# First gate pairs interleaved with their moving sums, three groups of elementwise work given to GpSimd, in a hybrid encoder layer on one core

## The chip, the cores and the metric

The kernel runs on one core of a Trainium2 chip. The metric is the device time of one execution in microseconds (us). Engines are called PE (TensorE), DVE (VectorE), ACT (ScalarE), POOL (GpSimd) and SP (SyncE).

## The reference

One layer of an encoder on 1024 tokens of width 1024, with 16 meta tokens ahead of them. What the change touches is the z part of the first projection, the two merge gates, and the gate/up projection of the SwiGLU:

```python
h = rmsnorm(h_res, norm1_w)
proj = h @ w_in
(q, k, v, z, b_raw, a_raw, sc_b, sc_c, sc_x, gate_a, gate_b) = split(proj)
o_dn = gated_deltanet_bidir(q, k, v, z, b_raw, a_raw, ...)   # gated by silu(z)
y_a = o_dn @ w_branch_dn
y_b = (sc_b * depthwise_conv_centred(sc_c * sc_x, sc_conv_w)) @ w_branch_sc
merged = sigmoid(gate_a) * y_a + sigmoid(gate_b) * y_b
h_res = h_res + merged @ w_out
h2 = rmsnorm(h_res, norm2_w)
gu = h2 @ w_gate_up
h_res = h_res + (silu(gu[..., :D_FF]) * gu[..., D_FF:]) @ w_down
out = rmsnorm(h_res, final_norm_w)[:, N_META:]
```

Everything is float32.

## The kernel before

**Arithmetic.** Each float32 operand of a large matmul is split in two: ACT casts a high part (`CAST`, L101 in `split`), DVE subtracts it from the value to get a low part (L102). Three matmuls per block of 128 rows give the product (high by high, high by low, low by high). `dense` (24 matmuls, 128x512 each) is such a product over eight blocks.

**Gate pairs.** The two merge gates are computed in pairs of units: for unit j = 3 to 7 (`GH` to `KT - 1`, n = 0 to 4), a block of gate A and one of gate B make one 2x2 block product with the 2x2 blocks B11, B12, B21, B22 of the activations. It is done with seven products instead of eight. On the weights' side stand A11, A12, A22 and sums S1 to S4; on the activations' side B11, B21, B22 and sums T1 to T4. `product` (12 matmuls, 128x512 each, L1440) is one of them. `pair_weights` loads a pair's raw weights (tiles `raw`) and gives two functions: `first` splits A11 and A12 (`wh`, `wl`), `second` splits A22 (`u_hl`; tile `w` for pair 0), forms S1 to S4 on DVE in place (`sums`, tiles `raw`) and splits these into tiles `mB` for even n and `mA` for odd n (`stationary2`). `pair` issues the products and combines the banks into two output tiles `s`. In order: A11·B11 and A12·B21 (both left half of the first output), S2·T2, S1·T1, S3·T3, S4·B22, A22·T4; the bank of A11·B11 is used again by S2·T2, S3·T3 and A22·T4.

**Moving sums.** `moving_sums` is a generator that forms T1 to T4 once, in steps, from high and low parts of the activations: float32 sums on DVE (128x2048, in tiles `mA` and `b`), the high CAST on ACT (L1457), and the low part on DVE (`b`). The tile `d_` holds differences of the low parts, once for T1 and again for T3.

**z heads.** `z_rows` does the last three heads of z (z0, z1, z2): two halves each, every one a `dense` into a bank from `psany`, then ACT's tanh of half (L1502) and on DVE one operation that reads the bank and ends the gate (L1504). `psany` rotates over all eight PSUM banks (tags m: two, e: three, d: three); `psz` rotates over m and e, `pss` gives d.

**Order.** From the z heads to the end of pair 0 the order on DVE, PE and ACT is the order of the source (`manual_schedule`, `border0`), and so it is on DVE alone in gate/up block 0. Elsewhere a list scheduler orders instructions when the program is built. Each engine runs its instructions strictly in that order.

**Gate/up.** The same scheme runs on the SwiGLU's projection. While the last row blocks are normalised and transposed, `second_half` forms the sums for T1, T2, T3 for a range of columns, `split_T2` splits T2 (`mA`) in two slices of columns (384 and 128 of each of four blocks, so 1536 and 512 elements a partition), and `form_T4` makes T4's float32 value in place of T2's with two operations on DVE (L179 and L228, tile `al`). T4's high CAST on ACT (`b`) and its low split on DVE follow.

Of the kernel before, what the change touches and what calls it, by code (L numbers as in the profile page):

```python
# [8 lines left out]
F32 = mybir.dt.float32  # L9
# [9 lines left out]
KT = 8  # L19
# [29 lines left out]
def encoder_layer(ctx: ExitStack, tc: tile.TileContext, x, meta, norm1_w, w_in, w_ba,  # L49
# [128 lines left out]
    def sub(out, a, b):  # L178
        nc.vector.tensor_tensor(out=out, in0=a, in1=b, op=ALU.subtract)  # L179
# [29 lines left out]
    def second_half(c, pts):  # L209
# [5 lines left out]
        sub(t2, b22, t1)  # L215
        sub(t3, b22, pts[0])

    def split_T2(c):

        b21h, b21l = (m[:, :, c].bitcast(F32) for m in mov["B21"])  # L220
        t2 = m32[2][:, :, c]
        split(*(m[:, :, c] for m in mov["T2"]), t2)

    def form_T4(c):
        b21h, b21l = (m[:, :, c].bitcast(F32) for m in mov["B21"])
        t2 = m32[2][:, :, c]
        sub(t2, b21h, t2)
        nc.vector.tensor_tensor(out=t2, in0=t2, in1=b21l, op=ALU.add)  # L228


    p_d = [dr.tile([P, SEQ], F32, name=f"p_d{i}") for i in range(KT)]
# [804 lines left out]
    with tc.tile_pool(name="st", bufs=1) as st:  # L1036
# [374 lines left out]
    s_hl, u_hl = [None, None], [None, None]  # L1411
    mov = {}

    def sums(rg, ru, s2, s4_, s3, s1):
        g0, g1, u0, u1 = rg[:, 0:4], rg[:, 4:8], ru[:, 0:4], ru[:, 4:8]
        nc.vector.tensor_tensor(out=s1, in0=u0, in1=u1, op=ALU.add)
        sub(s3, g0, u0)
        sub(s2, s1, g0)
        sub(s4_, g1, s2)

    def stationary2(j, ru, sa, sb, A_):

# [19 lines left out]
    def moving_sums():  # L1442

        c = [slice(C0 + META + 512 * i, C0 + META + 512 * i + 512) for i in range(2)]
        f = lambda m: m.bitcast(F32)
        h0, h1 = ([f(hx[0][:, 4 * i:4 * i + 4, cc]) for cc in c] for i in range(2))
        l0, l1, l2 = ([f(t[:, :, cc]) for cc in c] for t in low_tiles)
        for i in range(2):
            for j in range(2):
                mov[f"B{i + 1}{j + 1}"] = hx[0][:, 4 * i:4 * i + 4, c[j]], [hx[1][4 * i + k][:, c[j]] for k in range(4)]  # L1450
        for i, n in enumerate(("T1", "T2", "T3")):
            t = big(f"b{i}", [P, 2, 4, 512])
            mov[n] = t[:, 0], t[:, 1]
# [3 lines left out]
        high = lambda n, t: nc.scalar.copy(mov[n][0], t)  # L1457
# [12 lines left out]
        low_part("T2", t2)  # L1470
        yield
        sub(t3, h1[1], h0[1])
        sub(d_[:, a], l1[1], l0[1][:, a])
        sub(d_[:, b], l2[1], l0[1][:, b])
        add(t3, t3, d_)
        high("T3", t3)
        yield
        sub(t1, h1[0], t2)
        low_part("T3", t3)
        yield  # L1480
        t = big("b3", [P, 2, 4, 512])
# [14 lines left out]
    def z_rows(h):  # L1496

        sz = s4(SEQ)
        for sl in (left, right):
            po = psany()  # L1500
            dense(po, z_units[h - ZH], hx, C0 + META + sl.start, 512)
            nc.scalar.activation(sz[:, sl], po, AF.Tanh, scale=0.5)  # L1502
            yield
            nc.vector.scalar_tensor_tensor(out=sz[:, sl], in0=sz[:, sl], scalar=1.0, in1=po, op0=ALU.add, op1=ALU.mult)  # L1504
        nc.sync.dma_start(z_d[h], sz)
        yield
# [3 lines left out]
    def pair_weights(n, j):  # L1510

        s_hl[n % 2] = big(("mB", "mA")[n % 2], [P, 2, 2, KT, P])
        if n == 0:
            u = big("w2", [P, 2, 4, P])
            u_hl[0] = u[:, 0], u[:, 1]
        elif n == 1:
            u_hl[1] = [tp.tile([P, 4, P], F32R, tag="t2", name=uid("u_hl"), bufs=2) for _ in range(2)]
        gh, gl = wtiles([P, KT, P])
        rg, ru = (rawtile([P, KT, P]) for _ in range(2))
        nc.sync.dma_start(rg, w_in[unit(OGA + j * P)])  # L1520
        nc.sync.dma_start(ru, w_in[unit(OGB + j * P)])
        A_ = {"A11": (gh[:, 0:4], gl[:, 0:4]), "A12": (gh[:, 4:8], gl[:, 4:8])}

        def first():
            split(gh, gl, rg)

        def second():
            split(*u_hl[n % 2], ru[:, 4:8])
            A_["A22"] = u_hl[n % 2]
            sums(rg, ru, rg[:, 0:4], rg[:, 4:8], ru[:, 0:4], ru[:, 4:8])  # L1530
            stationary2(n, ru, rg, ru, A_)
        return A_, first, second

    def pair(n, j, A_, first, second):

        last = j == KT - 1
        o1, o2 = s4(), s4()
        bank = pss()
        if not last:
            if n:  # L1540
                first()
            product(bank, A_["A11"], "B11")
            nc.scalar.copy(o1[:, left], bank)  # L1543
            po = psz()
            product(po, A_["A12"], "B21")
            add(o1[:, left], po, o1[:, left])
            half_turn(o1[:, left])
        if last:
            first()
        if n:  # L1550
            second()
        bank2 = psz()
        if not last:
            product(bank, A_["S2"], "T2", True)
            nc.scalar.copy(o1[:, right], bank)
            product(bank2, A_["S1"], "T1")
            nc.scalar.copy(o2[:, right], bank2)
            product(bank, A_["S3"], "T3", True)
            add(o2[:, right], bank, o2[:, right])
            half_turn(o2[:, right])  # L1560
            product(bank2, A_["S4"], "B22", True)
            add(o1[:, right], bank2, o1[:, right])
            half_turn(o1[:, right])
            product(bank, A_["A22"], "T4", True)
            nc.scalar.activation(o2[:, left], bank, AF.Tanh, scale=0.5)
        else:
# [19 lines left out]
            half_turn(o1[:, right])  # L1586
        nc.sync.dma_start(ta_d[j], o1)
        nc.sync.dma_start(tb_d[j], o2)
        return o1
# [9 lines left out]
    next(sums_of_blocks)  # L1599
    next(z0)  # L1600
    next(z1)
    pair0 = pair_weights(0, GH)
    next(z1)
    pair0[1]()
    next(z1)
    pair0[2]()
    next(z2)
    next(sums_of_blocks)
    next(z2)
    next(sums_of_blocks)  # L1610
    next(sums_of_blocks)
    next(z2)
    next(sums_of_blocks)
    for n, j in enumerate(range(GH, KT)):
        o1 = pair(n, j, *(pair_weights(n, j) if n else pair0))
        if n == 0:
            border0.close()
# [182 lines left out]
    for j in range(NF):  # L1800
# [187 lines left out]
```

## Time and profile before

| | us |
|---|---|
| median of 3 runs | 2007.1 (2004.61 to 2007.71) |
| the profiled execution | 2003.46 |
| its span in the trace | 2001.7 |
| PE busy | 1974.2 (99%) |
| DVE busy | 1398.8 (70%) |
| ACT busy | 837.2 (42%) |
| POOL busy | 108.0 (5%) |
| mean granted TensorE clock | 0.996 |

The span is the time from the first to the last record of the trace, 1.8 us less than that execution's own time. The z heads and the first gate pairs lie between about 945 and 1005 us, gate/up block 0 between about 1363 and 1400 us. POOL has no work in either place.

### The profile page before, as it was taken

The page shows a single profiled execution, that of the slowest core. Times are in us where ns is not written, and L with a number is a line of the kernel's source. Part 1 is how long each engine was busy: PE and PEld are TensorE (multiplying, and loading weights), DVE is VectorE, ACT ScalarE, POOL GpSimd, SP SyncE. Part 2 cuts the span into 40 slices and gives each one's busy share as a digit, 9 for nine tenths or more (in the row PEclk, how much of TensorE's full clock was granted, in tenths as well). Part 3 has the DMA queues.
Part 4 walks back from the last instruction along what each step waited for, and adds up shares of the span by engine and source line. Part 5 has one row for each costly group of instructions (what it writes and reads, how often), then busy time and mean ns, then how long its engine had stood idle before and what let it go on. Part 6 is the DMA issues. An engine that isn't in the chain of part 4 may idle for free.

```text
span 2001.7 us, 31862 instructions
## 1 busy us (share of the span) xinstructions
PE 1974.2 (99%) x11999; PEld 1720.7 (86%) x11999; DVE 1398.8 (70%) x3020; ACT 837.2 (42%) x1964; POOL 108.0 (5%) x407
## 2 busy tenths in 40 slices
PE   9999999999999999999899999999999999999998
PEld 8999999999999999888688888887888888888887
DVE  6888688888888888844945544469866666656575
ACT  6472354636464646343344221224323333334344
POOL 2011101010101010100000000000000000000000
PEclk9999999999999999999999999999999999999999
DMA  3122221212222212222236743123666345477654
GB/s 133 65 90 74 59 86 59 75 59 75 59 75 59 86 59 65 75 85 91 94 112 239 248 151 112 63 85 107 240 231 216 140 150 188 157 276 244 193 170 172
DMA packets 124689, 251.00 MB, mean 125 GB/s; under 512 B 44981, under 2 KB 46438, under 8 KB 122103
## 3 DMA queue, kind: packets, MB, share of 16 engines
q1 hardware_dynamic: 123959, 247.92, 37.2%
q8 instruction: 94, 1.54, 0.3%
q10 hardware_dynamic: 576, 1.05, 0.1%
q14 instruction: 60, 0.49, 0.1%
HBM read 180.67 MB, written 68.25 MB: 124 GB/s over the span
## 4 chain that ended last, share of the span: by engine, by line
PE 47%; DVE 3%; ACT 1%; issue 1%; DMA 1%; SPq 0%; DVEq 0%; ACTq 0%
PE pd L1440 13%; PE pe L1440 6%; PE pm L1440 4%; PE pe L1894 1%; PE pe L1895 1%; PE pe L1896 1%; PE pd L1894 1%; PE pd L1895 1%; PE pd L1896 1%; PE pd L135 1%; PE pd L134 1%; PE pe L135 1%; PE pe L134 1%; PE pd L136 1%; PE pe L136 1%; PE pm L1895 1%
## 5 line engine op out<-in xcount | busy, mean ns | idle before, releaser
L341 PE MATMUL pm<-hTh,wh 128*128 128x320 f32 (+4 forms) x1264 | 434.2, 349 | 0.4 <-ACT hTh L1103 0.2
L341 PE MATMUL pm<-al,wh 128*128 128x320 f32 (+4 forms) x1264 | 433.6, 348 | 0.0
L341 PE MATMUL pm<-hTh,wl 128*128 128x320 f32 (+4 forms) x1264 | 431.7, 347 | 0.0
L341 PEld LDWEIGHTS pm<-hTh,wh 128*128 128x128 f32 x1264 | 236.7, 188 | 12.6 <-issue 1.3
L341 PEld LDWEIGHTS pm<-hTh,wl 128*128 128x128 f32 x1264 | 237.0, 188 | 10.9 <-issue 0.4
L341 PEld LDWEIGHTS pm<-al,wh 128*128 128x128 f32 x1264 | 236.9, 188 | 10.3
L102 DVE TENSOR_TENSOR al<-raw,ring_h 128x1024 fp32r<-128x1024 f32 x73 | 88.6, 1223 | 64.8 <-ACT ring_h L101 64.4
L101 ACT CAST ring_h<-raw 128x1024 fp32r<-128x1024 f32 x73 | 76.8, 1053 | 107.1 <-PE pe L1896 35.5
L363 DVE SCALAR_TENSOR_TENSOR kq<-ra,wc,kq 128x520 f32<-128x520 f32 x128 | 96.6, 755 | 4.9 <-ACT kq L393 4.0
L990 DVE TENSOR_TENSOR wl<-raw,wh 128x512 fp32r<-128x512 f32 x114 | 77.4, 689 | 31.1 <-ACT wh L993 30.6
L889 ACT ACTIVATE w<-pd,small 128x128 f32<-128x128 f32 x128 | 39.8, 363 | 125.0 <-PE pd L882 124.3
L101 ACT CAST wh<-raw 128x1024 fp32r<-128x1024 f32 x48 | 50.4, 1050 | 77.7 <-PE pd L135 18.7
L500 DVE TENSOR_TENSOR fP<-fP,tm 128x135 f32<-128x135 f32 (+23 forms) x248 | 71.7, 289 | 5.1
L496 DVE TENSOR_TENSOR tm<-fP,fN 128x135 f32<-128x135 f32 (+23 forms) x248 | 71.5, 288 | 4.4
L993 ACT CAST wh<-raw 128x512 fp32r<-128x512 f32 x114 | 67.4, 621 | 3.7 <-issue 3.6
L102 DVE TENSOR_TENSOR wl<-raw,wh 128x1024 fp32r<-128x1024 f32 x48 | 58.5, 1220 | 13.6 <-ACT wh L101 13.4
L1409 DVE TENSOR_TENSOR b<-pd,b 128x512 f32<-128x512 f32 x22 | 15.2, 690 | 66.2 <-PE pd L1440 66.2
L1831 ACT ACTIVATE b<-b 128x512 f32<-128x512 f32 x22 | 13.9, 632 | 113.3 <-DVE b L1409 113.3
L1440 PE MATMUL pd<-b_hl,wh 128*128 128x512 f32 x176 | 54.4, 390 | 0.0
L856 ACT ACTIVATE jk<-NP 128x128 f32<-128x128 f32 x64 | 19.9, 311 | 78.8 <-DVE NP L852 77.7
L1440 PE MATMUL pd<-b,mB 128*128 128x512 f32 x204 | 50.7, 398 | 1.1 <-ACT s L1543 1.1
L876 DVE SCALAR_TENSOR_TENSOR r<-pd,negEG,vS 128x128 f32<-128x128 f32 x120 | 36.7, 345 | 20.9 <-PE pd L866 20.5
(590 smaller groups left out, 4724.6 us busy)
## 6 DMA issues: line engine op xcount, KB each, us to landing
raw<-in_w_in_dram SPq DMA_DIRECT2D x72, 512.0 KB
raw<-in_w_gate_up_dram SPq DMA_DIRECT2D x44, 512.0 KB
sums<-in_w_down_dram SPq DMA_DIRECT2D x22, 512.0 KB
t_d<-sums SPq DMA_DIRECT2D x11, 1024.0 KB
raw<-s_d SPq DMA_DIRECT2D x44, 256.0 KB
raw<-t_d SPq DMA_DIRECT2D x44, 256.0 KB
act_d<-b SPq DMA_DIRECT2D x43, 256.0 KB
raw<-act_d SPq DMA_DIRECT2D x33, 256.0 KB
```

Source lines behind the costliest of these rows:

```text
L101: nc.scalar.copy(hi, src)
L102: nc.vector.tensor_tensor(out=lo, in0=src, in1=hi.bitcast(F32), op=ALU.subtract)
L134: mm(po[:m, :n], wh[:, k, :m], xhk[:, t0:t0 + n], start=(k == 0), stop=False)
L135: mm(po[:m, :n], wh[:, k, :m], xlk[:, t0:t0 + n], start=False, stop=False)
L341: mm(po[:, :n], ww[:, k], f(k)[:, t0:t0 + n], start=i == 0, stop=i == 3 * KT - 1)
L363: nc.vector.scalar_tensor_tensor(out=acc, in0=raw[:, h0 + t:h0 + t + hn], scalar=wc[:, t, col:col + 1], in1=acc, op0=ALU.mult, op1=ALU.add)
L496: nc.vector.tensor_tensor(out=tv, in0=fP[:, 0:r, j:j + 1].broadcast_to([P, r, n]), in1=fN[:, j:j + 1, j + 1:32].broadcast_to([P, r, n]), o ...
L500: nc.vector.tensor_tensor(out=fP[:, 0:r, j + 1:32], in0=fP[:, 0:r, j + 1:32], in1=tv, op=ALU.subtract)
L990: nc.vector.tensor_tensor(out=u[1][1][:, k], in0=u[2][:, k], in1=u[1][0][:, k].bitcast(F32), op=ALU.subtract)
L993: nc.scalar.copy(u[1][0][:, k], u[2][:, k])
L1440: mm(po, x[:, k], y, start=k + i == 0 and not add_to, stop=k == 3 and i == 2, skip_group_check=add_to)
L1895: mm(bank[t], h_[:, c], l_[:, hi], start=False, stop=False)
```

## The change

Three things are changed.

*z and the gate pairs.* `z_rows` takes its banks from `psz`. `pair` becomes a generator with stops behind A12·B21, S1·T1, S4·B22 and so on, and the source interleaves pairs 0 and 1 with the steps of the moving sums; S4·B22 stands ahead of S3·T3. The part of the weights' work with A22 and the sums is a function of its own (`block_sums`).

*To POOL, in that stage.* The sums S1 to S4 of pairs 0 and 1 (four operations 128x512 each), and the two subtractions into `d_` for T3 (128x1024 each), which are issued right behind T1's sum instead of after t3.

*To POOL, in gate/up.* `form_T4` runs on POOL, for each slice right behind that slice's split of T2; T4's split on DVE and ACT follows B22's and A22's.

```diff
+    def form_T4(c):
+        b21h, b21l = (m[:, :, c].bitcast(F32) for m in mov["B21"])
+        t2 = m32[2][:, :, c]
+        nc.gpsimd.tensor_tensor(out=t2, in0=b21h, in1=t2, op=ALU.subtract)
+        nc.gpsimd.tensor_tensor(out=t2, in0=t2, in1=b21l, op=ALU.add)
+
     def split_T2(c):
...
         split(*(m[:, :, c] for m in mov["T2"]), t2)
-
-    def form_T4(c):
-        b21h, b21l = (m[:, :, c].bitcast(F32) for m in mov["B21"])
-        t2 = m32[2][:, :, c]
-        sub(t2, b21h, t2)
-        nc.vector.tensor_tensor(out=t2, in0=t2, in1=b21l, op=ALU.add)
+        form_T4(c)
...
-    def sums(rg, ru, s2, s4_, s3, s1):
+    def sums(rg, ru, s2, s4_, s3, s1, engine=nc.vector):
         g0, g1, u0, u1 = rg[:, 0:4], rg[:, 4:8], ru[:, 0:4], ru[:, 4:8]
...
+        tt = engine.tensor_tensor
+        tt(out=s1, in0=u0, in1=u1, op=ALU.add)
+        tt(out=s3, in0=g0, in1=u0, op=ALU.subtract)
+        tt(out=s2, in0=s1, in1=g0, op=ALU.subtract)
+        tt(out=s4_, in0=g1, in1=s2, op=ALU.subtract)
...
         add(t1, t1, d_)
+        for p_, l_ in ((a, l1), (b, l2)):
+            nc.gpsimd.tensor_tensor(out=d_[:, p_], in0=l_[1], in1=l0[1][:, p_], op=ALU.subtract)
         high("T1", t1)
...
         sub(t3, h1[1], h0[1])
-        sub(d_[:, a], l1[1], l0[1][:, a])
-        sub(d_[:, b], l2[1], l0[1][:, b])
         add(t3, t3, d_)
...
         for sl in (left, right):
-            po = psany()
+            po = psz()
...
         def second():
+            stationary2(n, ru, rg, ru, A_)
+
+        def block_sums():
             split(*u_hl[n % 2], ru[:, 4:8])
             A_["A22"] = u_hl[n % 2]
-            sums(rg, ru, rg[:, 0:4], rg[:, 4:8], ru[:, 0:4], ru[:, 4:8])
-            stationary2(n, ru, rg, ru, A_)
+            sums(rg, ru, rg[:, 0:4], rg[:, 4:8], ru[:, 0:4], ru[:, 4:8], nc.gpsimd if n < 2 else nc.vector)
...
+            product(bank, A_["A11"], "B11")
+            nc.scalar.copy(o1[:, left], bank)
+            po = psz()
+            product(po, A_["A12"], "B21")
+            add(o1[:, left], po, o1[:, left])
+            half_turn(o1[:, left])
+            yield
+            if n:
+                second()
+            bank2 = psz()
+            product(bank, A_["S2"], "T2", True)
+            nc.scalar.copy(o1[:, right], bank)
+            product(bank2, A_["S1"], "T1")
+            nc.scalar.copy(o2[:, right], bank2)
+            yield
+            product(bank2, A_["S4"], "B22", True)
+            add(o1[:, right], bank2, o1[:, right])
+            half_turn(o1[:, right])
+            product(bank, A_["S3"], "T3", True)
+            add(o2[:, right], bank, o2[:, right])
+            half_turn(o2[:, right])
+            yield
+            product(bank, A_["A22"], "T4", True)
+            nc.scalar.activation(o2[:, left], bank, AF.Tanh, scale=0.5)
...
-    next(sums_of_blocks)
-    next(sums_of_blocks)
+    pair0 = pair(0, GH, *weights0)
+    weights1 = pair_weights(1, GH + 1)
+    next(pair0)
     next(z2)
     next(sums_of_blocks)
...
+    weights1[1]()
+    weights1[2]()
+    next(pair0)
+    next(sums_of_blocks)
+    next(pair0)
+    pair1 = pair(1, GH + 1, *weights1)
+    next(pair1)
+    next(sums_of_blocks)
+    next(pair0)
+    next(pair1)
+    border0.close()
...
             split(*mov["B22"], m32[0])
             block22(0, w0[1], w0[2])
-            form_T4(slice(0, 512))
+            split(*mov["T4"], m32[2])
         product(bank, A_["S3"], "T3", True)
         add(u3, bank, u3)
-        if j == 0:
-            split(*mov["T4"], m32[2])
```

On ACT, at the end of the z heads (`b_2081` is T3's high part, `b_2100` and `b_2112` T4's, the first `s_2101` or `s_2107` row is the copy of pair 0's A11·B11, and `s_2097` is z2). Before:

```order
L1502 ACTIVATE s_2097_12366<-pd_12367 128x512
L101 CAST wh_12539<-raw_12541 128x1024
L101 CAST wh_12659<-raw_12661 128x1024
L1457 CAST b_2081_12242<-b_2083_12244 128x2048
L1502 ACTIVATE s_2097_12366<-pd_12399 128x512
L1457 CAST b_2100_12427<-mA_12243 128x2048
L1543 COPY s_2101_12434<-pd_12436 128x512
```

And now:

```order
L1504 ACTIVATE s_2097_12368<-pm_12369 128x512
L1459 CAST b_2081_12242<-b_2083_12244 128x2048
L1504 ACTIVATE s_2097_12368<-pe_12399 128x512
L1573 COPY s_2107_12434<-pd_12436 128x512
L1510 ACTIVATE s_2107_12434<-s_2107_12434 128x512
L101 CAST wh_12428<-raw_12430 128x1024
```

The copy stood behind T4's high CAST and stands behind T3's now; the weights of the next pairs are cast after it.

On DVE, in the same place (`b_2083` holds t3 and `d_`, `mB` is the weights' sums of pair 0, `s_2097` is z2). Before:

```order
L179 TENSOR_TENSOR raw_12321<-raw_12321 128x512
L102 TENSOR_TENSOR mB_12317<-raw_12321,mB_12317 128x1024
L102 TENSOR_TENSOR mB_12317<-raw_12322,mB_12317 128x1024
L179 TENSOR_TENSOR b_2083_12244<-hTh 128x2048
L179 TENSOR_TENSOR b_2083_12244<-al_125,al_124 128x1024
L179 TENSOR_TENSOR b_2083_12244<-al_126,al_124 128x1024
L102 TENSOR_TENSOR wl_12540<-raw_12541,wh_12539 128x1024
L1409 TENSOR_TENSOR b_2083_12244<-b_2083_12244 128x2048
L1504 SCALAR_TENSOR_TENSOR s_2097_12366<-s_2097_12366,pd_12367 128x512
```

And now:

```order
L102 TENSOR_TENSOR w_2091_12320<-raw_12324,w_2091_12320 128x512
L1506 SCALAR_TENSOR_TENSOR s_2088_12292<-s_2088_12292,pe_12328 128x512
L102 TENSOR_TENSOR mB_12319<-raw_12323,mB_12319 128x1024
L102 TENSOR_TENSOR mB_12319<-raw_12324,mB_12319 128x1024
L179 TENSOR_TENSOR b_2083_12244<-hTh 128x2048
L1410 TENSOR_TENSOR b_2083_12244<-b_2083_12244 128x2048
L1506 SCALAR_TENSOR_TENSOR s_2097_12368<-s_2097_12368,pm_12369 128x512
```

The sums and `d_` are gone from between the low splits, the low splits still stand ahead of t3, and z2's operation reads a bank of tag m where it read one of tag d.

On DVE in gate/up block 0 (`al_14132` is the float32 of T2 and then T4, `b_2385` T4's low part). Before:

```order
L102 TENSOR_TENSOR w_2395_15042<-raw_14794,w_2395_15042 128x512
L179 TENSOR_TENSOR al_14132<-b_hl,al_14132 128x2048
L102 TENSOR_TENSOR u_hl_15123<-raw_14891,u_hl_15123 128x512
L228 TENSOR_TENSOR al_14132<-al_14132,b_hl 128x2048
L1409 TENSOR_TENSOR b_2364_14873<-pd_14915,b_2364_14873 128x512
L1416 TENSOR_TENSOR raw_14891<-raw_14891 128x512
L179 TENSOR_TENSOR raw_14891<-raw_14890,raw_14891 128x512
L102 TENSOR_TENSOR b_2385_14999<-al_14132,b_2385_14999 128x2048
```

And now:

```order
L102 TENSOR_TENSOR w_2395_15046<-raw_14794,w_2395_15046 128x512
L102 TENSOR_TENSOR b_2385_15003<-al_14132,b_2385_15003 128x2048
L1410 TENSOR_TENSOR b_2364_14873<-pd_14917,b_2364_14873 128x512
L102 TENSOR_TENSOR u_hl_15125<-raw_14891,u_hl_15125 128x512
L1418 TENSOR_TENSOR raw_14891<-raw_14891 128x512
L1419 TENSOR_TENSOR raw_14891<-raw_14890,raw_14891 128x512
```

T4's two operations are gone from DVE, and its low split has moved ahead.

More of the change, by code (lines that the diff above doesn't have):

```diff
@@ L1412, in encoder_layer @@
     mov = {}
-    def sums(rg, ru, s2, s4_, s3, s1):
+    def sums(rg, ru, s2, s4_, s3, s1, engine=nc.vector):
         g0, g1, u0, u1 = rg[:, 0:4], rg[:, 4:8], ru[:, 0:4], ru[:, 4:8]
[L1416 to L1419, printed above, removed]
+        tt = engine.tensor_tensor
[3 more added lines that the diff above has]
+        tt(out=s4_, in0=g1, in1=s2, op=ALU.subtract)
     def stationary2(j, ru, sa, sb, A_):
@@ L1527, in second, with pair @@
         def second():
+            stationary2(n, ru, rg, ru, A_)
+        def block_sums():
             split(*u_hl[n % 2], ru[:, 4:8])
             A_["A22"] = u_hl[n % 2]
-            sums(rg, ru, rg[:, 0:4], rg[:, 4:8], ru[:, 0:4], ru[:, 4:8])
-            stationary2(n, ru, rg, ru, A_)
-        return A_, first, second
-    def pair(n, j, A_, first, second):
+            sums(rg, ru, rg[:, 0:4], rg[:, 4:8], ru[:, 0:4], ru[:, 4:8], nc.gpsimd if n < 2 else nc.vector)
+        return A_, first, block_sums, second
+    def pair(n, j, A_, first, block_sums, second):
         last = j == KT - 1
-        o1, o2 = s4(), s4()
+        o1, o2 = outs[n] = s4(), s4()
         bank = pss()
[L1539 to L1547, printed above, removed]
         if last:
             first()
-        if n:
+            block_sums()
             second()
[L1552 to L1566, printed above, removed]
+            bank2 = psz()
             product(bank, A_["S2"], "T2")
@@ L1586, in pair @@
             half_turn(o1[:, right])
+        else:
+            if n > 1:
+                first()
+                block_sums()
+            product(bank, A_["A11"], "B11")
[7 more added lines that the diff above has]
+                second()
+            bank2 = psz()
+            product(bank, A_["S2"], "T2", True)
[12 more added lines that the diff above has]
+            nc.scalar.activation(o2[:, left], bank, AF.Tanh, scale=0.5)
         nc.sync.dma_start(ta_d[j], o1)
         nc.sync.dma_start(tb_d[j], o2)
-        return o1
+        yield
+    outs = {}
     sums_of_blocks = moving_sums()
@@ L1601, in encoder_layer @@
     next(z1)
-    pair0 = pair_weights(0, GH)
+    weights0 = pair_weights(0, GH)
     next(z1)
-    pair0[1]()
+    weights0[1]()
+    weights0[2]()
     next(z1)
-    pair0[2]()
+    weights0[3]()
     next(z2)
@@ L1609, in encoder_layer @@
     next(z2)
-    next(sums_of_blocks)
-    next(sums_of_blocks)
+    pair0 = pair(0, GH, *weights0)
+    weights1 = pair_weights(1, GH + 1)
+    next(pair0)
     next(z2)
     next(sums_of_blocks)
[L1614 to L1617, printed above, removed]
+    weights1[1]()
[9 more added lines that the diff above has]
+    border0.close()
+    for _ in pair1:
+        pass
+    for n, j in enumerate(range(GH + 2, KT), 2):
+        for _ in pair(n, j, *pair_weights(n, j)):
+            pass
+    o1 = outs[KT - 1 - GH][0]
     warm2 = keep.tile([P, 1], F32, name="warm2")
```

## Prediction

> **What bounds the kernel now.** I read the page first, its busy times, to see whether there is slack at all.
>
> ```profile
> span 2001.7 us, 31862 instructions
> PE 1974.2 (99%) x11999; PEld 1720.7 (86%) x11999; DVE 1398.8 (70%) x3020; ACT 837.2 (42%) x1964; POOL 108.0 (5%) x407
> ```
>
> TensorE (PE) is busy for 1974.2 of 2001.7 us, so all idle time together is 27.5 us, and no change that leaves the matmuls alone gains more than that plus what half-clock stretches cost. The product count stays the same. So I asked for the waits in the two places that the diff touches: the z heads with the first gate pairs (945 to 1005 us) and gate/up block 0 (1363 to 1400 us). First place, "waiter <- waited for: us in total, times, longest":
>
> ```profile
> PE pd L1440 <- DVE s L1504: 7.7, 2, 5.9
> PE pd L1440 <- ACT s L1543: 1.1, 1, 1.1
> ```
>
> The timeline of PE there (start, us, tile, and in brackets the idle time and its releaser), then windows of 3.41 us, whose last columns but two give the granted clock:
>
> ```profile
> 968.07 0.50 PE L134 MATMUL pd<-hTh,wh 128*128 128x512 f32 x1 [0.19 <-ACT wh L101]
> 969.33 0.51 PE L136 MATMUL pd<-hTh,wl 128*128 128x512 f32 x1 [0.53 <-DVE wl L102]
> ...
> 985.12 0.39 PE L1440 MATMUL pm<-hTh,wl 128*128 128x512 f32 x1
> 991.38 0.77 PE L1440 MATMUL pd<-hTh,wh 128*128 128x512 f32 x1 [5.88 <-DVE s L1504]
> ...
> 998.56 0.50 PE L1440 MATMUL pd<-hTh,wh 128*128 128x512 f32 x1 [1.85 <-DVE s L1504]
> ...
> 1000.43 4.33 PE L1440 MATMUL pd<-b,mB 128*128 128x512 f32 x12 [1.14 <-ACT s L1543]
> 1004.60 0.62 PE L1440 MATMUL pe<-b,mB 128*128 128x512 f32 x2
> ```
>
> ```profile
> 986.21:989.62 3.41, 0.00 (x0) 0.00 (x0) 3.41 (x3) 0.38 (x1) 0.00 (x0) 1.00 0.04 18
> 989.62:993.03 3.41, 1.65 (x4) 1.39 (x5) 3.41 (x3) 2.36 (x2) 0.00 (x0) 0.50 0.00 0
> 999.86:1003.27 3.41, 2.83 (x7) 2.26 (x8) 3.41 (x4) 1.31 (x3) 0.00 (x0) 0.50 0.22 89
> ```
>
> At full rate a matmul starts every 0.227 us here (the same trace has 12 of them in 2.72). Between the last matmul of pair 0's A12·B21 (985.12, so its slot ends at 985.35) and the first S1·T1 (1004.60) stand only 26 matmuls: 12 of pair 1's A11, two of pair 2's, 12 of S2·T2. These need 5.9 us and took 19.25: 13.4 us are lost, and about 1.1 more at z2's start (968.07, 969.33). That is **14.5 us** in stage 1. A window that follows one with almost no matmuls runs at 0.50, and a full one costs half of 3.41, 1.7 us.
>
> The reason for the 5.88 and 1.85 is that pair 1's A11 wants a bank that z2 holds until VectorE (DVE) reaches L1504, and DVE has wide sums ahead of it. The rows of DVE and of ScalarE (ACT):
>
> ```profile
> 957.63 2.29 DVE L1409 TENSOR_TENSOR mA<-mA,b 128x2048 f32<-128x2048 f32 x1
> 959.96 2.29 DVE L179 TENSOR_TENSOR mA<-hTh,mA 128x2048 f32<-128x2048 f32 x1
> 962.28 2.36 DVE L1409 TENSOR_TENSOR mA<-mA,al 128x1024 f32<-128x1024 f32 x2
> ...
> 974.33 0.69 DVE L102 TENSOR_TENSOR w<-raw,w 128x512 fp32r<-128x512 f32 x1
> ...
> 980.47 2.36 DVE L102 TENSOR_TENSOR mB<-raw,mB 128x1024 fp32r<-128x1024 f32 x2 [1.11 <-ACT mB L101]
> ...
> 984.95 2.35 DVE L179 TENSOR_TENSOR b<-al,al 128x1024 f32<-128x1024 f32 x2
> ...
> 988.35 2.29 DVE L1409 TENSOR_TENSOR b<-b 128x2048 f32<-128x2048 f32 x1
> ```
>
> ```profile
> 964.68 1.92 ACT L1457 CAST b<-mA 128x2048 fp32r<-128x2048 f32 x1 [2.81 <-DVE mA L1409]
> ...
> 966.98 1.04 ACT L101 CAST wh<-raw 128x1024 fp32r<-128x1024 f32 x1
> ...
> 979.38 2.00 ACT L101 CAST mB<-raw 128x1024 fp32r<-128x1024 f32 x2 [5.66 <-DVE raw L179]
> ...
> 990.67 1.90 ACT L1457 CAST b<-b 128x2048 fp32r<-128x2048 f32 x1 [4.09 <-DVE b L1409]
> 992.48 0.59 ACT L1502 ACTIVATE s<-pd 128x512 f32<-128x512 f32 x1
> ...
> 999.81 0.58 ACT L1543 COPY s<-pd 128x512 f32<-128x512 f32 x1
> ```
>
> In stage 2 PE waits for T4: DVE forms it with the two operations that the change takes away (1380.90, 1383.70), ACT casts it, PE starts it.
>
> ```profile
> 1366.70 1.22 DVE L102 TENSOR_TENSOR wl<-raw,wh 128x1024 fp32r<-128x1024 f32 x1
> ...
> 1370.88 0.69 DVE L102 TENSOR_TENSOR mA<-al,mA 128x512 fp32r<-128x512 f32 x1 [0.24 <-ACT mA L101]
> ...
> 1380.90 2.28 DVE L179 TENSOR_TENSOR al<-b_hl,al 128x2048 f32<-128x2048 f32 x1
> ...
> 1383.70 2.28 DVE L228 TENSOR_TENSOR al<-al,b_hl 128x2048 f32<-128x2048 f32 x1
> ```
>
> ```profile
> 1374.32 2.88 PE L1440 MATMUL pd<-mA,mB 128*128 128x512 f32 x12
> ...
> 1387.97 0.50 PE L1440 MATMUL pd<-b,w 128*128 128x512 f32 x1 [2.61 <-ACT b L101]
> ```
>
> With the half-clock window behind it, the smaller waits and the weights of block 1, stage 2 loses some 6.8 us between 1363 and 1400, counted as above.
>
> **The price on GpSimd (POOL).** The change gives POOL 14 wide tensor_tensors: two of 1024, eight of 512, two of 1536 and two of 512 elements a partition. The trace shows only four wide ones on POOL, all near the start, with DVE's rows of the same time:
>
> ```profile
> 15.63 2.52 POOL L1118 TENSOR_TENSOR wl<-raw,wh 128x512 fp32r<-128x512 f32 x2 [14.04 <-ACT wh L1117]
> 23.33 2.98 POOL L1118 TENSOR_TENSOR wl<-raw,wh 128x512 fp32r<-128x512 f32 x2 [5.19 <-ACT wh L1117]
> ```
>
> ```profile
> 22.43 0.16 DVE L168 SCALAR_TENSOR_TENSOR ss<-ss 128x1 f32<-128x1 f32 x1
> 22.62 1.29 DVE L1089 SCALAR_TENSOR_TENSOR xr<-xr,ss,w1row 128x1024 f32<-128x1024 f32 x1
> ...
> 24.07 0.99 DVE L167 SCALAR_TENSOR_TENSOR ss<-ss 128x1 f32<-128x1 f32 x1
> 25.10 1.22 DVE L168 SCALAR_TENSOR_TENSOR ss<-ss 128x1 f32<-128x1 f32 x1
> ```
>
> A 512 costs 1.26 us undisturbed. So I price a 1024 at 2.4 (2.5 at most, as two of 512) and a 1536 at 3.5 (3.8 at most). The second pair took 2.98: the first of it stood until DVE's L1089 (22.62, two tensors from SBUF) was over at 23.9. And DVE's tiny L168, 0.16 us at 22.43, took 1.22 at 25.10 and ended with POOL's second operation (23.33 + 2.98 = 26.31). So a wide POOL operation and a DVE operation with two inputs in SBUF exclude each other, and they take turns.
>
> The Trainium skill, "SBUF — State Buffer", section "Who interferes with whom", states the same against this change: the port pair that DVE and GpSimd share is an exclusive lock, not a split of bandwidth. This trace agrees by the 1.22 in place of 0.16; by a reading without that lock the sum below would be that of the first rival. "GPSIMD Engine Reference", section 3.1, gives 4497 ns for a tensor_tensor of 2048 on GpSimd; an estimate from that page is 2.25 for a 1024, which would take 0.3 us off stage 1; no run here shows that width.
>
> **Stage 1, part by part.** *Banks apart.* z2 moves to banks that pair 1's A11 does not want: the 5.88 and 1.85 behind L1504 go. What is next late is S2·T2 of pair 0, which now follows A12 directly and, as before, needs ACT's copy of A11's left half out of the same bank. On ACT that copy stands behind T3's high CAST and a tanh of z2, so behind t3 on DVE. I reckon its time below.
>
> *d_ on POOL.* It moves from 984.95 (2.35 on DVE) to right behind DVE's add of 957.63, which ends at 959.92. DVE goes straight on to t2 (2.29, till 962.2); POOL's first takes its turn till 964.6, DVE's first add of T2 (1.18) till 965.8, POOL's second till 968.2, DVE's second add till 969.4 instead of 964.64: **+4.7 us**. T2's high CAST (964.68) and z2's weight CAST (966.98) are queued behind that on ACT, and PE's z2 waits for the weight. Before, z2 was nearly on time (0.19 idle), so the 4.7 land on PE: z2 starts near 972.7, A12 ends near 990.1.
>
> *Block sums on POOL.* They start after the u low split (974.33 + 0.69, so 975.0, +4.7 = 979.7). Four of 1.27 make 5.1: 984.8. DVE has nothing to take from the port then, since the next thing on it is mB's low split, which waits for these sums and is queued ahead of t3. The first mB CAST takes 1.0, the two low splits 2.36: 988.2. Then t3 and its add (988.35), 2.29 each: 992.7. T3 CAST 1.90, tanh 0.59 and copy 0.58, overlapping by about 0.1 each: 995.5. PE starts S2·T2 near 995.7, so it idles 995.7 − 990.1 = **5.6 us**. That the sums left DVE gains nothing here: a 512 takes 1.27 on POOL against 0.69 on DVE (974.33), and DVE waits for it.
>
> *Products interleaved.* S4·B22 now comes right behind S1·T1 in the same bank and must wait for ACT's copy: about 0.3 to notice and 0.58 to copy, 0.9. With pair 1's A11 and A12 in between, T4 of pair 0 waits for nothing. Pair 1's S2·T2 waits some 1.3 for its own weights (sums, CAST, low split), and small ones add 0.5; these two are estimates from the same rows, strung together in the new order. DMAs: the only moves on SyncE are stores of pair 0's output ahead of loads for pair 3, whose slots come free earlier; nothing waits for them, and if the cover went it would be one load, under 4 us.
>
> Sum: 4.7 + 1.1 (z2's small waits as before) + 5.6 + 0.9 + 1.3 + 0.5 = 14.1 us at full clock. Two stalls of about 5 us are long enough to leave a window of 3.41 almost empty more often than not; none would cost 0, three windows 5.1; I take one and a half, 2.6. That is 16.7 against 14.5: **+2.2 us**, with ends of −0.4 and +4.7.
>
> **Stage 2.** DVE loses 2 × 2.28 = 4.56 us. POOL's first slice starts when T2's first low split is over, 1366.1, and holds the port for 3.5: the split of the next weights (1366.70) starts at 1369.7, 3.0 late. POOL's add takes the next turn, 1370.9 to 1374.4, and the sums of the last row block, which feed T2's second slice, stand behind it, 5.5 late. S2·T2 (1374.32) had 2.7 us in hand behind that slice's low split (1370.88 + 0.69), so S2·T2 starts 2.5 to 3 late; the second slice (two of 1.26, each a turn) adds 2, so S3·T3 is 4.5 late. T4's CAST is then early enough, and the 2.61 at 1387.97 and its half-clock window go. In place of 6.8 us I get 4.5, plus the small waits for block 1's weights (2.2) and one half window (1.7): 8.4, **+1.6 us**, ends +0.5 and +2.6.
>
> **Total.** The profiled execution took 2003.46 us, 1.8 more than its span. 2003.46 + 2.2 + 1.6 = 2007.3. The median of the runs shown is 3.6 higher (2007.1), so I expect 2007.1 + 3.8 = **2010.9 us**. With the ends of the two terms this case spans 2007 to 2014. About 0.2%, 4 us, is what a measurement can tell from no change.
>
> **Rivals.** *The ports don't clash for these shapes, or clash little.* Then d_ and T4 are hidden on POOL. Stage 1: z2 on time, S2·T2 still 5.6 late by the queue on ACT, 0.9, 1.3, 0.5 and 1.1 as above, 9.4, plus one and a quarter windows: 11.5, −3.0. Stage 2: only small waits, 1.4 instead of 6.8, −5.4. Together −8.4: 1998.7, faster. For it: 108 us of POOL work beside DVE at 70% already. Against it: the rows at 24.07 and 25.10. It decides if DVE's T2 adds still end near 964.6. Chance 0.25.
>
> *Wide or strided operations on POOL cost more per element than its 512.* The new ones run over two or four rows with gaps, and no row has a width above 512. At half as much again (3.6 for a 1024, 5.3 for a 1536) d_ adds 2.4 more in stage 1, stage 2's turns add some 2 more: 2010.9 + 4.4 = 2015.3, slower. It decides from about 3.0 us for a 1024. Chance 0.20.
>
> *DVE keeps the port while its instructions follow each other closely, and POOL waits for gaps.* d_ isn't wanted before t3, so stage 1 goes as in the first rival, −3.0; T4 in stage 2 comes as late as before, 0. 2004.1, no measurable change. For it: from 957.63 to 964.64 DVE has no gap. Against it: at 25.10 POOL's second operation went ahead of a waiting DVE. Chance 0.08. My forecast has 0.47.
>
> **Chances.** The forecast lies on the border of 4 us: of its 0.47, 0.22 slower, 0.24 same, 0.01 faster. First rival 0.23 faster, 0.02 same; second 0.20 slower; third 0.06 same, 0.02 faster. Faster 0.26, same 0.32, slower 0.42. The range runs from 1998 (about a tenth lies below, in the first rival) to 2016 (about a tenth above, in the second).
>
> **What would show it.** Right: POOL's d_ rows of 2.3 to 2.5 each that begin when a DVE operation ends, T2's adds on DVE ending near 969, z2 on PE starting near 972.7, an idle time of about 5.6 ahead of S2·T2 released by ACT's copy, no wait for L1506 (the old L1504); in stage 2 the weights' low split about 3 late and no wait of 2.6 for T4. Wrong: d_ overlapping t2 at its full 2.29, z2 at 968, S2·T2 without the idle time, or T4's POOL operations running beside DVE's rows of unchanged length.

## The result and the profile after

The changed kernel takes 2009.97 us (median of 20 runs, 2007.26 to 2011.87), the kernel before 2006.69 (20 runs, 2004.61 to 2010.64). The ratio is 1.0013, 95% interval 1.0007 to 1.0019: 1.4 to 3.8 us slower. The forecast was 2010.9.

The page's span and busy times (the profiled execution took 2009.70 us):

```profile
span 2008.0 us, 31870 instructions
PE 1977.5 (98%) x11999; PEld 1720.0 (86%) x11999; DVE 1399.4 (70%) x3008; ACT 836.7 (42%) x1964; POOL 138.8 (7%) x421
```

DVE has 12 instructions fewer and is as busy as before (1399.4 against 1398.8): what left it came back as waiting inside its rows. Stage 1 on DVE and POOL; a row of "x2" holds two instructions:

```profile
960.86 2.29 DVE L179 TENSOR_TENSOR mA<-hTh,mA 128x2048 f32<-128x2048 f32 x1
963.19 6.63 DVE L1410 TENSOR_TENSOR mA<-mA,al 128x1024 f32<-128x1024 f32 x2
...
986.16 2.36 DVE L102 TENSOR_TENSOR mB<-raw,mB 128x1024 fp32r<-128x1024 f32 x2 [6.00 <-ACT mB L101]
```

```profile
961.05 7.69 POOL L1465 TENSOR_TENSOR b<-al,al 128x1024 f32<-128x1024 f32 x2 [134.26 <-DVE mA L1410]
979.65 1.29 POOL L1418 TENSOR_TENSOR raw<-raw 128x512 f32<-128x512 f32 x1 [10.91 <-DVE w L102]
...
1003.49 2.20 POOL L1418 TENSOR_TENSOR raw<-raw 128x512 f32<-128x512 f32 x1 [18.45 <-DVE u_hl L102]
```

T2's two adds, 2.36 us before, take 6.63 while POOL forms `d_`. POOL's 512 takes 1.29 at 979.65, where DVE has no operation with two inputs in SBUF, and 2.20 at 1003.49, where it has. DVE stands for 6.00 us ahead of `mB`: it waits for ACT's CAST, and that for POOL's sums. PE in the same stage, and two windows of its clock (the last number but two):

```profile
973.23 0.79 PE L134 MATMUL pm<-hTh,wh 128*128 128x512 f32 x1 [4.67 <-ACT wh L101]
...
996.01 4.44 PE L1442 MATMUL pd<-b,mB 128*128 128x512 f32 x12 [3.42 <-ACT s L1573]
1000.29 2.89 PE L1442 MATMUL pe<-b,mB 128*128 128x512 f32 x12
1003.85 0.50 PE L1442 MATMUL pe<-hTh,mB 128*128 128x512 f32 x1 [0.68 <-ACT s L1585]
...
1024.66 2.57 PE L1442 MATMUL pd<-b,mA 128*128 128x512 f32 x10 [0.68 <-DVE mA L102]
```

```profile
971.80:975.20 3.40, 1.93 (x4) 1.11 (x5) 2.80 (x4) 3.40 (x6) 0.00 (x0) 0.50 0.00 0
975.20:978.60 3.40, 3.40 (x10) 2.63 (x9) 3.40 (x4) 0.41 (x1) 0.00 (x0) 0.50 0.65 220
```

z2 starts after 4.67 us of idle time, then runs at half clock; S2·T2 waits 3.42 for the copy of A11 and runs its 12 matmuls in 4.28 us instead of 2.72. No wait names z2's banks any more. Stage 2, POOL and DVE, then the starts of S2·T2, S3·T3 and A22·T4 on PE:

```profile
1368.90 3.51 POOL L221 TENSOR_TENSOR al<-b_hl,al 128x1536 f32<-128x1536 f32 x1 [357.36 <-PE pd L1442]
1372.49 4.36 POOL L222 TENSOR_TENSOR al<-al,b_hl 128x1536 f32<-128x1536 f32 x1
```

```profile
1369.28 4.21 DVE L102 TENSOR_TENSOR wl<-raw,wh 128x1024 fp32r<-128x1024 f32 x1
...
1374.12 3.27 DVE L179 TENSOR_TENSOR al<-al,b_hl 128x512 f32<-128x512 f32 x1
...
1380.24 4.18 DVE L102 TENSOR_TENSOR s<-al,s 128x1024 fp32r<-128x1024 f32 x2
```

```profile
1379.78 2.79 PE L1442 MATMUL pd<-mA,mB 128*128 128x512 f32 x11 [0.23 <-DVE mA L102]
...
1387.27 2.77 PE L1442 MATMUL pd<-b,mB 128*128 128x512 f32 x11 [0.44 <-DVE b L102]
...
1392.88 3.02 PE L1442 MATMUL pd<-b,w 128*128 128x512 f32 x12
```

The 2.61 ahead of T4 is gone; in its place DVE's two-input operations beside POOL's 1536 are 2.6 to 3.0 us longer (4.21 for 1.22, 3.27 for 0.69), and the two beside its 512 together 1.8 (4.18 for 2.36).

**A table by place.** All kernels here but the one that measures the price alone issue 11999 matmuls. The start of the n-th one, less its start in the kernel before, tells where time was lost or won. The columns are four stretches of the kernel before, in us of its trace: stage 1 (966 to 1030), the pairs behind it (1030 to 1073), stage 2 (1362 to 1412), and a place at 1488 to 1504 that the prediction did not know. In the fourth place PE waits for DVE, and DVE for a load of w_down. The names are those of the experiments below.

```
                          stage 1   pairs 1-3   stage 2   1488-1504
changed kernel              +0.8       +1.1       +1.5       +2.2
e1_d_vector                 -0.1       +1.1       +1.8       -0.1
e2_T4_vector                +1.6       +1.1       +1.1       +1.4
e3_sums_vector              -3.0       +1.1       +2.0       +4.0
e4_copy_first               -4.2       +1.1       +2.1       +1.4
e5_order_only               -2.5       +1.1       +0.8       +3.9
e6_no_gpsimd_copy_first     -8.3       +1.0       +0.6       +1.1
e7_banks_only               +1.7        0.0       +1.1       +1.4
e8_d_gpsimd                 -4.9       +1.1       +1.0       -0.2
e9_T4_gpsimd                -8.7       +1.0       +1.5       +0.4
```

Each line is one execution, and the one of before was quick in the last two columns: five kernels with its own stage 2 (e2, e5 to e8) show +0.6 to +1.1 there, 0.9 in the mean. The last column goes from −0.2 to +4.0, also at +1.4 in e7, which differs from before by one line far away. So it scatters by itself, and I count none of it to the change; why that load comes late in some executions stays open. The columns don't add up to the whole difference: ahead of 940 us the executions already differ from the one of before by 0.0 to 1.9 us. Nor is stage 1 exact to a few tenths: e2, whose stage 1 is that of the changed kernel, has +1.6 there and not +0.8.

### The profile page after: what moved, and what is told of

It is laid out like the page before. It is cut to its first block, busy times and chain, and to the rows that moved or that the text cites. A ratio compares the mean times of both kernels' runs of the same rounds, so it can differ in the third digit from the quotient of the medians.

```text
span 2008.0 us, 31870 instructions
## 1 busy us (share of the span) xinstructions
PE 1977.5 (98%) x11999; PEld 1720.0 (86%) x11999; DVE 1399.4 (70%) x3008; ACT 836.7 (42%) x1964; POOL 138.8 (7%) x421
## 4 chain that ended last, share of the span: by engine, by line
PE 43%; DVE 4%; DMA 2%; issue 2%; ACT 1%; POOL 0%; SPq 0%; DVEq 0%; POOLq 0%; ACTq 0%
PE pd L1442 12%; PE pe L1442 5%; PE pm L1442 3%; PE pe L1918 1%; PE pe L1919 1%; PE pe L1917 1%; PE pd L1918 1%; PE pd L1919 1%; PE pd L1917 1%; PE pd L136 1%; PE pe L136 1%; PE pd L135 1%; PE pe L135 1%; PE pe L134 1%; PE pd L134 1%
## 5 line engine op out<-in xcount | busy, mean ns | idle before, releaser
L342 PEld LDWEIGHTS pm<-al,wh 128*128 128x128 f32 x1264 | 237.4, 189 | 10.4
```

Of the source, the lines that this page charges most:

```text
L342: mm(po[:, :n], ww[:, k], f(k)[:, t0:t0 + n], start=i == 0, stop=i == 3 * KT - 1)
```

## The experiments

The theory is that of the prediction: a wide POOL operation and a DVE operation with two inputs in SBUF exclude each other and take turns, so what POOL takes off DVE comes back as waiting; and S2·T2 hangs on a copy that is late in ACT's queue. Times are medians; the kernel before, run beside them, had 2006.4 to 2006.9 (2006.7 beside the changed kernel), so a difference between kernels of two series is good to about half a us.

**The price by itself.** A program of loads and elementwise operations only; its sections are named in the expectation.

> Not the layer: only a series of operations on loaded data, which leaves the whole computation out, to measure the disputed price. In order: POOL alone with 512, 1024, 1536 (4x384) and 2048 elements a partition; DVE alone with two SBUF inputs of 1024; four POOL operations of 1024 beside twelve such DVE operations, each waiting for its own predecessor; the same with outputs that don't depend on each other; four POOL operations of 1024 beside sixteen DVE operations with one input in PSUM. Theory: POOL alone 1.27 for 512, 2.3 to 2.5 for 1024, about 3.5 for 1536 and 4.5 for 2048; beside DVE's two-input operations the two take turns, so while POOL works each DVE row of 1.2 shows 3.4 to 3.7 and each POOL row as well; beside the operations with a PSUM input both keep their own times. Rival one (no exclusion, POOL is only slow): both keep their own times in all sections. Rival two (DVE keeps the port while its instructions follow each other): with independent outputs POOL's first row lasts until DVE's twelve are over, some 13 us.

Groups by line and shape (count, busy us, mean ns): POOL alone first, then the section in which all operations of an engine write one tile (its 13 on DVE hold one from the section of DVE alone), the one with four tiles in turn, and that with a PSUM input.

```profile
L78 POOL TENSOR_TENSOR w<-w,v 128x2048 f32<-128x2048 f32 x2 | 9.0, 4495 | 0.2
L78 POOL TENSOR_TENSOR w<-w,v 128x1536 f32<-128x1536 f32 x2 | 6.8, 3417 | 0.1
L75 POOL TENSOR_TENSOR vp<-va,vb 128x1024 f32<-128x1024 f32 x1 | 2.3, 2341 | 0.1
L75 POOL TENSOR_TENSOR vp<-va,vb 128x512 f32<-128x512 f32 x1 | 1.3, 1262 | 0.0
```

```profile
L81 DVE TENSOR_TENSOR vd<-va,vb 128x1024 f32<-128x1024 f32 x13 | 24.0, 1847 | 0.4
L75 POOL TENSOR_TENSOR vp<-va,vb 128x1024 f32<-128x1024 f32 x4 | 12.9, 3230 | 5.8 <-DVE va L87 5.6
```

```profile
L81 DVE TENSOR_TENSOR vd<-va,vb 128x1024 f32<-128x1024 f32 x12 | 22.3, 1928 | 0.0
L75 POOL TENSOR_TENSOR vp<-va,vb 128x1024 f32<-128x1024 f32 x4 | 13.2, 3333 | 10.2 <-DVE va L87 10.2
```

```profile
L84 DVE SCALAR_TENSOR_TENSOR vd<-vb,bank 128x512 f32<-128x512 f32 x16 | 11.0, 687 | 0.5
L75 POOL TENSOR_TENSOR vp<-va,vb 128x1024 f32<-128x1024 f32 x4 | 9.4, 2354 | 9.6 <-DVE va L87 9.4
```

Alone POOL takes 1.26, 2.34, 3.42 and 4.50 us. Beside two-input operations its 1024 takes 3.23 with one output tile and 3.33 with four; beside operations that read PSUM it keeps 2.35, and they keep their 0.69. Within the two middle sections the four POOL operations alternate with four DVE operations of 3.2 to 3.4 each, and the other DVE operations stay at 1.2. Both rivals fall: there is an exclusion, and DVE does not keep POOL out (13 us for POOL's first row was that rival's sign). The Trainium skill, "GPSIMD Engine Reference", section 3.1, gives 4497 ns for the 2048; the 4495 here agree. The 2.25 that the prediction estimated from it for a 1024 was 2.34.

**One part undone at a time.** The first puts `d_` back:

```diff
-        for p_, l_ in ((a, l1), (b, l2)):
-            nc.gpsimd.tensor_tensor(out=d_[:, p_], in0=l_[1], in1=l0[1][:, p_], op=ALU.subtract)
...
         sub(t3, h1[1], h0[1])
+        sub(d_[:, a], l1[1], l0[1][:, a])
+        sub(d_[:, b], l2[1], l0[1][:, b])
```

> The changed kernel with one part undone: the two subtractions into d_ for T3 are on DVE again, behind t3. Theory (a wide POOL operation and a DVE operation with two inputs in SBUF exclude each other): DVE's two adds of T2 take 2.36 us together again instead of 6.6, z2 starts on PE with under 0.5 us of idle time instead of 4.7 and without the half-clock window behind it, A12 ends some 6.5 us earlier. T3's chain on DVE is 2.35 longer, so the idle time ahead of S2·T2 grows from 3.4 to about 8 us. Together 1 to 3 us less than the changed kernel, so about 2007.5 to 2009. Rival (POOL is merely slow, and the adds of T2 are late for another reason, the new order of the queues): the adds stay at 6.6, z2 stays 4.7 late, and the 2.35 come on top, about 2012.

2008.24 us, ratio to before 1.0007 (0.9997 to 1.0016). DVE and PE:

```profile
963.35 2.36 DVE L1410 TENSOR_TENSOR mA<-mA,al 128x1024 f32<-128x1024 f32 x2
```

```profile
969.14 0.50 PE L134 MATMUL pm<-hTh,wh 128*128 128x512 f32 x1 [0.38 <-ACT wh L101]
...
994.24 5.49 PE L1442 MATMUL pd<-b,mB 128*128 128x512 f32 x12 [7.66 <-ACT s L1573]
```

The adds are back at 2.36 and z2 is on time, and the idle time comes up again ahead of S2·T2: 7.66 where 8 was expected. Most of what `d_` on POOL cost was hidden behind that wait.

The second undoes gate/up (`form_T4` on `nc.vector` behind `block22`, T4's split behind S3·T3, as in the kernel before):

> The changed kernel with its gate/up part undone: form_T4 on DVE as before, in one piece behind B22's and A22's splits. Theory: the next weights' low split is back at 1.22 us instead of 4.2, the T1, T3 and B22 products are not late any more, and the waits for T4 (2.6 us and a half-clock window) are back: stage 2 loses 6.8 us instead of some 8.3, so the whole is 1 to 2 us below the changed kernel, about 2008.5. Rival (POOL's T4 was hidden and all of the loss lies in stage 1): taking it back costs 5 us, about 2015.

2008.28 us, ratio 1.0013 (1.0003 to 1.0022). The median falls by 1.7 us as expected, but the ratio is that of the changed kernel, so the total alone settles nothing. The table does more: stage 2 is at +1.5 to +2.1 in the five kernels with T4 on POOL (1.8 in the mean), and at 0.9 in the mean of the five without. The price is about 0.9, and 1.5 against the one execution of before. The rival, 5 us the other way, falls.

The third gives S1 to S4 back to DVE:

```diff
-            sums(rg, ru, rg[:, 0:4], rg[:, 4:8], ru[:, 0:4], ru[:, 4:8], nc.gpsimd if n < 2 else nc.vector)
+            sums(rg, ru, rg[:, 0:4], rg[:, 4:8], ru[:, 0:4], ru[:, 4:8], nc.vector)
```

> The changed kernel with S1 to S4 of pairs 0 and 1 on DVE again. DVE stood idle for 6 us while POOL formed those of pair 0. Theory: four operations of 0.6 us on DVE in place of 5.4 on POOL, so mB's split, t3, T3's CAST and the copy ahead of S2·T2 come 2.8 us earlier; the idle time of 3.4 ahead of S2·T2 falls to about 0.6 and the half-clock window behind it goes or shrinks; pair 1's sums leave the T4 adds alone but take 2.4 on DVE. 2.5 to 4.5 us below the changed kernel, 2005.5 to 2007.5. Rival (DVE's load is what counts, so each operation off DVE helps): 1 to 3 us slower than the changed kernel.

2006.32 us, ratio 0.9997 (0.9988 to 1.0007), 3.7 below the changed kernel: more work on the busier engine, and faster.

```profile
994.16 3.04 PE L1442 MATMUL pd<-b,mB 128*128 128x512 f32 x12 [1.36 <-ACT s L1573]
```

The wait ahead of S2·T2 falls from 3.42 to 1.36 (0.6 was expected), and its half-clock window goes (3.04 for 12).

**One instruction moved.** T3's high CAST goes behind the copy on ACT (a stop more in each generator, and one `next` more of each in the source's order; behind them a copy and a weight's CAST on ACT change places too):

```diff
         add(t3, t3, d_)
+        yield
         high("T3", t3)
...
             nc.scalar.copy(o1[:, left], bank)
+            if n == 0:
+                yield
...
     next(pair0)
+    next(sums_of_blocks)
+    next(pair0)
     next(z2)
```

> The changed kernel with one instruction moved on ACT: the copy of pair 0's A11 stands ahead of T3's high CAST instead of behind it (A11's half turn behind it), everything else the same. Theory (S2·T2 waits only for that place in ACT's queue): its idle time falls from 3.4 to under 0.5 us, the half-clock window after it (1.6 us) goes, about 5 us below the changed kernel: 2004 to 2006. Rival (T3's chain itself is what everything waits for, the queue only shows it): the wait moves to S3·T3, which then waits 3 to 5 us for T3's low part, and the time stays within 1.5 us of the changed kernel.

2004.51 us, ratio 0.9989 (0.9980 to 0.9999), 5.5 below the changed kernel. PE around S2·T2:

```profile
993.35 0.39 PE L1442 MATMUL pm<-hTh,wl 128*128 128x512 f32 x1
993.57 2.88 PE L1442 MATMUL pd<-b,mB 128*128 128x512 f32 x12
996.29 2.88 PE L1442 MATMUL pe<-b,mB 128*128 128x512 f32 x12
1000.13 0.50 PE L1442 MATMUL pe<-hTh,mB 128*128 128x512 f32 x1 [0.96 <-ACT s L1588]
```

The 3.42 are gone, and no wait for T3 took their place; what is left there is 0.96 ahead of S4·B22. The wait was the queue's, not T3's.

**The order without POOL, and the banks alone.** The first undoes `d_`, the sums and T4 together, and leaves the banks and the order of the change:

> The changed kernel with all three groups of POOL work on DVE again (d_, S1 to S4, T4 as before): what is left of the change is z2's banks, the interleaved order and S4·B22 ahead of S3·T3. Theory: z2 on time, no wait for z2's banks; T3's chain is what S2·T2 waits for through ACT's queue (mB's split done near 981, t3, d_ and the add 7 us, CAST, tanh and copy 3: about 992.7 against A12's end at 986, 6 to 7 us idle and one or two half-clock windows), stage 1 loses 11 to 13 us instead of 14.5 before, stage 2 the same as before: 2003 to 2006, that is 4 to 6 below the changed kernel. Rival (POOL's help was worth something, the order is what costs): above the changed kernel, 2011 or more.

2005.07 us, ratio 0.9991 (0.9982 to 1.0000).

```profile
991.77 5.49 PE L1441 MATMUL pd<-b,mB 128*128 128x512 f32 x12 [5.06 <-ACT s L1572]
```

z2 is on time, and S2·T2 waits 5.06 (6 to 7 were expected) and runs at half clock. Against 2009.97 the three groups on POOL together cost 4.9 us (4.6, each taken against the kernel before run beside it). Undone singly they give 1.7, 1.7 and 3.7; the parts of stage 1 share the wait ahead of S2·T2 and don't add up. The other is the kernel before with one line changed:

```diff
-            po = psany()
+            po = psz()
```

> The kernel before with one line of the change: z_rows takes its banks from psz, nothing else moved. Theory (the wait of 5.88 us for z2's banks covers the one behind it, for ACT's copy of A11): the two waits for L1504 go, pair 1's A11 runs at 986, and PE then stands until the copy at 999.8, idle for over 10 us in one piece; S2·T2 starts within 1.5 us of where it did, so the time is within 2 us of the kernel before, 2004.5 to 2008.5. Rival (the bank is what stage 1 waits for, as the table of waits says): 7.7 us of waits and a half-clock window go, 6 us or more faster.

2006.46 us, ratio 0.9998 (0.9989 to 1.0008): no change.

```profile
987.84 0.50 PE L1440 MATMUL pd<-hTh,wh 128*128 128x512 f32 x1 [0.67 <-ACT wh L101]
989.73 0.50 PE L1440 MATMUL pd<-hTh,wl 128*128 128x512 f32 x1 [1.16 <-DVE wl L102]
...
1001.68 5.49 PE L1440 MATMUL pd<-b,mB 128*128 128x512 f32 x12 [7.87 <-ACT s L1543]
```

The 7.7 us of waits for z2's banks became one of 7.87 for the copy; of the more than 10 expected in one piece, 1.8 went to pair 1's weights ahead of it (0.67 and 1.16). PE's longest wait of this stage before was cover for another.

**A version that beats both, and POOL in it.** From e5, with the copy first as in e4, t3's first subtraction ahead of `mB`'s splits and T3's low part ahead of T4's first subtraction on DVE (the part in `moving_sums`; the stop in `pair` is that of e4, and the source calls the generators three times more):

```diff
         sub(t3, h1[1], h0[1])
+        yield
         sub(d_[:, a], l1[1], l0[1][:, a])
         sub(d_[:, b], l2[1], l0[1][:, b])
         add(t3, t3, d_)
+        yield
         high("T3", t3)
         yield
-        sub(t1, h1[0], t2)
         low_part("T3", t3)
+        sub(t1, h1[0], t2)
         yield
```

> The version that the theory points to: no new work on POOL, z2's banks and the order of the change, the copy of A11 ahead of T3's CAST on ACT, t3's first subtraction ahead of mB's splits and T3's low part ahead of T4's first subtraction on DVE. Theory: no wait of over 1 us is left in stage 1 (it loses 2 to 4 us instead of 14.5), stage 2 as before: 1994 to 1998. Rival (the DVE work that is now all on one engine comes late somewhere behind, at T3's low part or at T4): a wait of 3 us or more moves there, 2000 or more.

1998.40 us, ratio 0.9957 (0.9944 to 0.9971): 8 us below the kernel before, with nothing new on POOL. The waits of PE between 945 and 1040 us (total, times, longest):

```profile
PE pd L1441 <- ACT mA L101: 1.2, 1, 1.2
PE pd L1441 <- DVE mA L102: 1.2, 1, 1.2
PE pe L1441 <- ACT s L1588: 1.0, 1, 1.0
PE pm L134 <- ACT wh L101: 0.5, 1, 0.5
PE pm L136 <- DVE wl L102: 0.5, 1, 0.5
```

The time is 0.4 above what was expected, and two waits of over 1 us are left where none was: pair 1's weights come late twice by 1.2. By the starts of the matmuls, stage 1 still loses 6.4 us and not 2 to 4. Giving it back `d_` on POOL, and then instead T4 on POOL:

> The best version so far (1998.4) with one group given to POOL again: the two subtractions into d_, right behind T1's sum. DVE has 2.35 us less to do. Theory: the two adds of T2 take 6.6 us instead of 2.36, z2 starts 4.2 us later and a half-clock window of 1.7 follows: 4 to 6.5 us slower than that version, 2002.5 to 2005. Rival (in the better order the delay of the adds is taken up by slack): within 1.5 us of it.

> The best version so far (1998.4) with the change's gate/up part: T4 formed on POOL in two slices. DVE has 4.56 us less to do there. Theory: the same as in the changed kernel, +1.5 in that stage (1 to 2.5 counting the spread), 1999.5 to 2001. Rival (stage 2's loss came from stage 1's delay): 4 to 5 us faster, 1994.

2002.97 us (ratio to before 0.9979, 0.9970 to 0.9989) and 2000.12 us (0.9962, 0.9948 to 0.9977). `d_` costs 4.6 us (4.0, each taken against the kernel before run beside it) where nothing hides it, though it takes 2.35 us off DVE:

```profile
963.00 6.64 DVE L1409 TENSOR_TENSOR mA<-mA,al 128x1024 f32<-128x1024 f32 x2
```

```profile
973.06 0.50 PE L134 MATMUL pm<-hTh,wh 128*128 128x512 f32 x1 [4.49 <-ACT wh L101]
```

T4 costs 1.7 by the medians (1.1, taken so); the two intervals overlap, so that is a direction, not a size.

## Why the prediction was right, step by step

- *The exclusion and the turns*: right, and shown by the program that measures it. The price of a 1024 (2.4) was 2.34, of a 1536 (3.5) 3.42. The `d_` rows of 2.3 to 2.5 named as a sign did not show: a row holds its wait for the turn, so they came as 7.69 for two.
- *`d_` on POOL, +4.7*: the adds grew by 6.63 − 2.36 = 4.3, and PE's idle time ahead of z2 was 4.67.
- *S2·T2 stays late by ACT's queue, 5.6*: the cause is shown by e4. The idle time was 3.42 and not 5.6. The start was as reckoned (996.01, less the 0.7 that this execution was late by then, against 995.7), but z2 ran at half clock ahead of it, so A12 ended later and the wait was shorter. The sum counted that half-clock window on top of the wait; it lay inside it. e2, with the same stage 1, shows this: there z2 ran slow for fewer matmuls, the wait was 4.36 and S2·T2 started at the same place (996.86, less the 1.55 that execution was late by then: 995.3 in both). That term was too large. The windows were too small: by the starts of the matmuls stage 1 loses 15.5 us now (16.7 reckoned; before 14.7, 14.5 reckoned), of it 10.4 at waits (14.1 reckoned) and 5.1 in matmuls that were slow without a wait (2.6 reckoned).
- *S4·B22 behind S1·T1, 0.9*: 0.68. *Pair 1's weights, 1.3*: 0.68. *z2's small waits, 1.1*: they did not come back.
- *A term left out*: S4·B22 ahead of S3·T3 was priced for pair 0 alone. Behind stage 1, every kernel with the new order loses 1.0 to 1.1 us in the table and e7, with the old one, nothing. No table of waits shows it: in the changed kernel it lies in products whose first two matmuls come 0.1 to 0.3 us late in all, S4·B22 (1045.27 and 1064.78, 0.4 together) and A22·T4 (1036.58, 1050.73 and 1070.06, 0.5 together). Each now follows directly the product that used its bank, S1·T1 or S3·T3; before, another product stood between. That this is the cause was not tried.
- Stage 1 with what follows it: 0.8 + 1.1 = 1.9 against +2.2, and 2.7 in e2's execution. The stage itself was reckoned too slow by 1.4 and what follows it left out at 1.1; that these nearly cancel is luck.
- *Stage 2, +1.6*: +1.5 against the execution that the sum was made against, about +0.9 against the mean. The next weights' low split was reckoned to start at 1369.7 and be 3.0 late; its row grew by 3.0. S3·T3 was to be 4.5 late; its first matmul began at 1386.33 and its second at 1387.27, which less the 2.6 that this execution was late by then is 4.0 and 4.7 behind the same two before (1379.76 and 1379.99). The half-clock window counted there did not come. By the starts of the matmuls the stage loses 5.7 us before and 7.2 now (1362 to 1412 us), where 6.8 and 8.4 were reckoned: both were about 1.2 too high, and the difference held.
- *Rivals*: the ports clash (first rival out), wide operations cost no more per element (second out), DVE does not keep the port (third out).
- The forecast of 2010.9 lay at the border of 4 us and the outcome 0.9 below it: +3.3 by the medians, within what was called the same.

## What to carry to other kernels

Before giving elementwise work to GpSimd, look at what VectorE does in the same microseconds: with two inputs in SBUF, each wide GpSimd operation delays it by about GpSimd's own, longer time (2.0 us for a 1024 that takes 2.34 alone), and three kernels here are faster for having work back on the busier engine (e3 and e5 against the changed kernel, e6 against e8). And a wait in the table says what ended last, not what would end next: changing the bank that PE waited 5.88 us for, alone, gained nothing; the wait for the copy behind it went when that copy came first in its queue.

## What had not been expected of the hardware

With one output tile, a DVE row that gives POOL a turn takes 3.25 us, less than the two times alone (2.34 + 1.23 = 3.57): a POOL operation of 1024 costs DVE 2.0 us, and T2's adds lost 4.3 us to two of them rather than 4.7. And the half speed behind the same wait was not the same each time: in the changed kernel the clock was 0.50 for all of 971.80 to 978.60, behind z2's 4.67 us; in e8, behind 4.49 us, it was this:

```profile
972.60:976.00 3.40, 2.42 (x6) 1.69 (x7) 2.96 (x2) 2.84 (x5) 0.00 (x0) 0.69 0.20 39
976.00:979.40 3.40, 3.40 (x13) 2.75 (x13) 3.40 (x5) 0.00 (x0) 0.00 (x0) 0.81 0.67 270
```

A mean of 0.69 and then 0.81 is half speed for 0.62 of the first 3.40 us and 0.38 of the second, together 3.4 us, one window where the changed kernel had two. What decides between one and two, no run here shows.
